# A planner's durations for TensorE products, by width, type and layout of the operands, in a two-block network

## The chip, the cores and the metric

The kernel runs on one core of one Trainium2 chip. The metric is the device time of one execution in microseconds, as the median of several runs. TensorE is called PE here, VectorE DVE, ScalarE ACT, GpSimd POOL, and SyncE SP; SP issues the DMAs.

## The reference

Two transformer-like blocks follow each other on one sequence of 1024 tokens of 1024 features, all in float32.

```python
def hybrid_layer(x, ...):                       # first block
    h = rmsnorm(x, norm1_w)
    proj = h @ w_in                             # q,k,v of two mixers, a gate, two scalars a head
    o_a = gated_delta_rule(qa, ka, va, g, beta) # 4 heads of 128, a recurrence over chunks
    o_b = dilated_attention(qb, kb, vb)         # 8 heads of 64, bands of dilation 1, 4 and 16
    x = x + concat([o_a, o_b]) @ w_out
    u = causal_dwconv(rmsnorm(x, norm2_w) @ w_up, ffn_conv_w)
    return x + (silu(gate) * up) @ w_down       # 2816 wide

def second_block(x, ...):
    proj = rms_norm(x) @ w_in                   # u, v, value, gate: 512 columns each
    a_out = spatial_gating(u_a, v_a, ...)       # chunks of 128 tokens
    b_out = conformer_conv(val_b, gate_b, ...)  # causal convolution with 31 taps, norm, silu
    x = x + concat([a_out, b_out]) @ w_out
    return rms_norm(x + square(relu(rms_norm(x) @ w_ff1)) @ w_ff2)   # 4096 wide
```

## The kernel before

Nearly all products of activations and weights are made in fp32r with operands split into a high and a low part: a product of two float32 matrices is three TensorE products (`mm3`: low x high, high x low, high x high). A tile is 128 rows by 512 columns (half the tokens), one PSUM bank; sums over 1024 features are 24 products. Smaller matrices (the recurrence, the attention's values, the second block's convolution) are multiplied as float32.

**The order is planned at build time.** The program is a set of generator tasks: one for the input projections (`proj1`), one a chunk of the recurrence (`gdn_intra`, with `gdn` for the state), one a head for the scan that finds the attention's maxima (`dil_scan`) and one a head for the attention itself (`dil_pv`), the dense parts (`proj_out`, `ffn`), the convolution (`conv31`, `conv_ln`), and small ones that evacuate a PSUM bank or split a weight. A task yields the engine on which it goes on and a condition. `Weaver.run` (L137) holds a planned clock for each engine. It takes the next task, lets it emit its instructions up to its next yield, and each instruction adds its planned duration to its engine's clock by `cost` (L124). What is emitted is the order of each engine's queue, and the hardware keeps it; nothing of the plan's times is left in the program, only the order and the semaphores.

A TensorE task may be taken if it is due within 50 ns of PE's planned clock, and of those the one with the lowest priority number and then the oldest is taken. A task of another engine is taken if it is due within 100 ns of PE's clock and its engine is planned not more than 2.5 or 6 us ahead (L150). A result passes between engines after a planned latency (`LAT`, L95: 200 ns from PE, 140 from ACT, 130 from DVE) and 230 ns more on the way from ACT or DVE to PE (`TOPE`). The planned durations of ACT, DVE, POOL and DMAs stand in `act`, `tt`, `ts`, `stt`, `ptt` and `dma`: ACT 52 or 94 ns and 0.833 a column, DVE 75 to 130 ns and 1.042 a column, a DMA 475 ns of issue, then 650 ns and its bytes by 360 a nanosecond behind the one before it, and 900 ns to land.

The parts that the steps below go through:

- Projections are filler with high priority numbers (`QP0`, `QP1`, `VP`: 8). `in_steps` (L594) lets go after every two of the eight k, so after six products. `ps_dil` holds q and k of the attention (512 columns), `ps_dv` its v (256 columns).
- The recurrence goes over eight chunks, two in work at a time. A chunk makes some 17 steps between PE and ACT or DVE (`ps_gcb`, `ps_A`, `ps_L`, `ps_T`, `ps_pU`, `ps_G`, `ps_w`), then `gdn` forms `ps_u`, `ps_S`, `ps_o`, and `ps_ot` transposes the result. Its fp32 products appear twice in the records.
- The scan (`ps_S` from arR) and the attention (`ps_T` from arR scores, `ps_O` values) work on heads whose q and k were written to DRAM (`qd`, `kd`) and are read again and split by `dil_split` (L1204) on ACT and DVE, in one queue with the band's additions on DVE and the exponentials on ACT. Six of the eight heads are read twice; two are kept from the scan. Scores of the first pattern use contiguous columns as the stationary operand, those of the second every eighth column (`slice(g + 4 * x, S, 8)`). `dil_pv` keeps three groups of scores ahead (`LA` = 3). The out projection's weights come only after it.
- Buffers come from two arenas; a task that asks for one (`room`) goes on when a planned release has made room.
- In the second block, `conv31` runs 31 taps over 4 groups of channels on DVE; for the last group three taps go to PE (`ps_c`) with diagonal matrices that ACT makes. `conv_ln` then transposes and centres (`ps_ct`), 1500 ns (`CLL`) after the planned end of the taps. `ps_v` and `ps_u` are projections beside it, `ps_sg` the gating, `ps_out` the out projection.

Of the kernel before, what the change touches and what calls it, by code (L numbers as in the profile page):

```python
# [247 lines left out]
def cols(ap):  # L248
    n = 1
    for d in ap.shape[1:]:  # L250
        n *= d
    return n
# [6 lines left out]
class Prog(Weaver):  # L259
# [10 lines left out]

    def mm(self, out, lhsT, rhs, start, stop, loose=False):
        n, m = cols(rhs), cols(lhsT)
        if rhs.dtype == F32:
            c = max(1.667 * n, 213.0 if m > 64 else 107.0)
        elif rhs.dtype == F32R:
            c = max(0.417 * n, 107.0 if m > 64 else 56.0)
        else:
            c = max(0.417 * n, 28.0)
        self.cost("PE", c)
        kw = {"skip_group_check": True} if loose else {}  # L280
        self.nc.tensor.matmul(out, lhsT, rhs, start=start, stop=stop, **kw)  # L281
# [5 lines left out]

    def tp(self, out, in_):
        k = in_.shape[0]
        self.cost("PE", 107.0)  # L290
        self.nc.tensor.transpose(out, in_, self.ident[:k, :k])

    def tpacc(self, out, in_, start):

        self.cost("PE", 107.0)
        self.nc.tensor.matmul(out, in_, self.ident, start=start, stop=True, is_transpose=True, skip_group_check=True)

    def act(self, out, in_, func=AF.Copy, bias=None, scale=None, accum=None):
# [304 lines left out]
    def proj1(self):  # L603
# [49 lines left out]
        for part in range(3):  # L653
            for blk in range(2):
                w = yield from self.pop(q)
                if first:
                    yield "PE", after(*hev[0])
                    self.warm = True
                got = {}
                for mm, hf in ((0, 0), (1, 0), (0, 1), (1, 1)) if first else ((0, 0), (0, 1), (1, 0), (1, 1)):  # L660
                    if first and hf:
                        yield "PE", after(*hev[1])
                    if not hf:
                        got[mm] = yield from rawr.get("PE")
                    h, rs = blk * 2 + mm, got[mm]
                    ps = self.psum("in1")
                    self.gemm_fm(ps, w, mm * P, hT[hf])
                    if not hf:
                        self.cost("POOL", 100.0)
                        nc.gpsimd.memset(rs.ap[:, 0:3], 0.0)  # L670
                    e = self.evac("ACT", lambda d=rs.ap[:, 3 + hf * H:3 + hf * H + H], ps=ps: self.act(d, ps))
                    if hf:
                        posts.append(self.spawn(self.conv4(part, h, rs, rawr, accr, vsr, e), prio=3, eng="DVE"))
                    self.hold = True
                    yield "PE"
                first = False
                self.put(hl, w)
# [1438 lines left out]
```

## Time and profile before

| | |
|---|---|
| median of 3 runs | 2617.27 us (2617.18 to 2620.52) |
| the profiled execution | 2619.11 us |
| its span, first to last instruction | 2617.3 us |
| TensorE busy | 2540.3 us, 97% |
| VectorE, ScalarE, GpSimd busy | 1370.7, 807.9, 121.1 us |
| mean granted clock of TensorE | 0.987 of full speed |

A row of the timeline is a run of like instructions: its start, its length, engine, line, output and inputs, count, and in brackets how long the engine stood before it and what ended that. All matmuls stand on the lines of the helpers (L281 `mm`, L291 `tp`, L296 `tpacc`), so they are told apart by the name of their output. The records of overlapping products are longer than the distance of their starts; the distance is what a product costs. A granted clock of 1.00 is 2.4 GHz, half of it is 1.2 GHz.

### The profile page before, as it was taken

To read this page: it belongs to the slowest core of one execution; us is meant where nothing else is said; L and a number is where in the kernel's file an instruction comes from. 1 tells how busy PE (TensorE), PEld (TensorE's weight loads), DVE (VectorE), ACT (ScalarE), POOL (GpSimd) and SP (SyncE) were. 2 spreads that over 40 slices of the span, in tenths; PEclk is the share of its full clock that TensorE was granted. 3 is DMA by queue.
4 is the path that set the end of the run, shared out by engine and by line. 5 is a ranking of instruction groups with operands and counts; after the bars stand their busy time and mean duration, and the time that the engine had idled before them with its cause. 6 is when DMAs were issued, how large, how long until landed. Compare 5 with 4: busy or idle time off the path is not lost.

```text
span 2617.3 us, 31361 instructions
## 1 busy us (share of the span) xinstructions
PE 2540.3 (97%) x13001; PEld 2180.4 (83%) x13001; DVE 1370.7 (52%) x1868; ACT 807.9 (31%) x1306; POOL 121.1 (5%) x245
## 2 busy tenths in 40 slices
PE   7999999988989999999999999989999999999998
PEld 6888999988978888888888888877788888888887
DVE  5441343454654555555555567969554444444444
ACT  5322443453541422222222235253232121212122
POOL 1010000000000000000000001050000000000000
PEclk9999999998989999999999999999999999999999
DMA  5232222232441111111111113102211111111111
GB/s 189 71 104 85 84 67 62 80 80 69 106 130 57 41 49 49 49 50 50 49 50 49 50 66 101 61 9 90 71 41 57 41 57 41 57 41 57 41 49 65
DMA packets 175164, 170.80 MB, mean 65 GB/s; under 512 B 25985, under 2 KB 148254, under 8 KB 175022
## 3 DMA queue, kind: packets, MB, share of 16 engines
q1 hardware_dynamic: 175022, 168.80, 21.2%
q8 instruction: 102, 1.67, 0.3%
q14 instruction: 40, 0.33, 0.0%
HBM read 145.50 MB, written 23.23 MB: 64 GB/s over the span
## 4 chain that ended last, share of the span: by engine, by line
PE 61%; issue 28%; DVE 4%; ACT 3%; DMA 2%; POOL 2%; SPq 0%; POOLq 0%; ACTq 0%; DVEq 0%
PE ps_up L281 18%; PE ps_dn L281 9%; PE ps_in L281 5%; PE ps_out L281 5%; PE ps_vg L281 3%; PE ps_dil L281 3%; PE ps_T L281 2%; ACT arF L311 2%; PE ps_S L281 2%; PE ps_z L281 2%; PE ps_O L281 2%; PE ps_dv L281 2%; DVE arF L327 2%; PE ps_pU L281 1%; PE ps_G L281 1%
## 5 line engine op out<-in xcount | busy, mean ns | idle before, releaser
L281 PE MATMUL ps_up<-arR 128*128 128x512 f32 x3648 | 831.5, 389 | 0.0
L281 PEld LDWEIGHTS ps_up<-arR 128*128 128x128 f32 x3648 | 684.5, 188 | 142.1
L315 DVE TENSOR_TENSOR arR<-arF,arR 128x1024 fp32r<-128x1024 f32 (+3 forms) x283 | 347.6, 1236 | 610.0 <-ACT arR L311 609.5
L281 PE MATMUL ps_dn<-arR 128*128 128x512 f32 x2592 | 591.8, 389 | 0.0
L311 ACT ACTIVATE arR<-arF 128x1024 fp32r<-128x1024 f32 (+3 forms) x297 | 311.2, 1071 | 852.3 <-PE ps_dn L281 394.3
L281 PEld LDWEIGHTS ps_dn<-arR 128*128 128x128 f32 x2592 | 486.4, 188 | 101.0
L315 DVE TENSOR_TENSOR arF<-arF,ps_dn 128x512 f32<-128x512 f32 x416 | 279.6, 684 | 183.2 <-PE ps_dn L281 183.2
L327 DVE SCALAR_TENSOR_TENSOR arF<-arF,pcol 128x1024 f32<-128x1024 f32 (+1 forms) x276 | 311.4, 1149 | 22.5 <-ACT arF L311 17.5
L311 ACT ACTIVATE arF<-arF 128x1024 f32<-128x1024 f32 (+3 forms) x158 | 134.8, 860 | 272.5 <-DVE arF L315 138.5
L281 PE MATMUL ps_out<-arR 128*128 128x512 f32 x768 | 182.2, 398 | 2.7 <-DVE arR L315 2.7
L281 PEld LDWEIGHTS ps_out<-arR 128*128 128x128 f32 x768 | 146.7, 192 | 34.4 <-DVE arR L315 3.7
L311 ACT ACTIVATE arF<-ps_up 128x512 f32<-128x512 f32 x152 | 89.5, 589 | 187.0 <-PE ps_up L281 187.0
L281 PE MATMUL ps_in<-arR 128*128 128x512 f32 x576 | 137.7, 399 | 0.0
L281 PEld LDWEIGHTS ps_in<-arR 128*128 128x128 f32 x576 | 109.4, 192 | 23.9
L315 DVE TENSOR_TENSOR arF<-arF 128x1024 f32<-128x1024 f32 (+4 forms) x91 | 89.1, 979 | 28.8 <-ACT arF L311 14.8
L281 PE MATMUL ps_dil<-arR 128*128 128x512 f32 x384 | 97.4, 403 | 0.0
L281 PE MATMUL ps_vg<-arR 128*128 128x512 f32 x384 | 88.3, 390 | 0.0
L281 PEld LDWEIGHTS ps_vg<-arR 128*128 128x128 f32 x384 | 71.8, 188 | 14.8
L281 PEld LDWEIGHTS ps_dil<-arR 128*128 128x128 f32 x384 | 71.7, 192 | 14.2
L281 PE MATMUL ps_O<-arF 128*128 128x128 f32 (+2 forms) x384 | 69.9, 328 | 12.2 <-ACT arF L311 6.8
L315 DVE TENSOR_TENSOR arF<-ps_G,csq 128x512 f32<-128x512 f32 x48 | 33.1, 690 | 90.8 <-PE ps_G L281 90.8
L315 DVE TENSOR_TENSOR arF<-arF,ps_out 128x512 f32<-128x512 f32 x64 | 43.5, 683 | 62.1 <-PE ps_out L281 62.1
(185 smaller groups left out, 2037.2 us busy)
## 6 DMA issues: line engine op xcount, KB each, us to landing
arF<-in_w_ff_dram SPq DMA_DIRECT2D x64, 512.0 KB
arF<-in_w_up_dram SPq DMA_DIRECT2D x44, 512.0 KB
arF<-in_w_in_dram SPq DMA_DIRECT2D x12, 1024.0 KB
arF<-in_w_down_dram SPq DMA_DIRECT2D x22, 512.0 KB
arF<-in_x_dram SPq DMA_DIRECT2D x16, 512.0 KB
arF<-in_w_out_dram SPq DMA_DIRECT2D x16, 512.0 KB
arF<-in_w_in_dram SPq DMA_DIRECT2D x16, 512.0 KB
arF<-kd SPq DMA_DIRECT2D x28, 256.0 KB
```

The costliest lines, as they stand in the source:

```text
L281: self.nc.tensor.matmul(out, lhsT, rhs, start=start, stop=stop, **kw)
L311: self.nc.scalar.activation(out, in_, func, **kw)
L315: self.nc.vector.tensor_tensor(out, a, b, op)
L327: self.nc.vector.scalar_tensor_tensor(out, a, s, b, op0, op1)
```

## The change

Four planned durations of TensorE products are replaced. A load figure, 112 ns for a stationary operand of more than 64 columns and 56 otherwise, bounds the cost from below in place of 107 and 56 (twice that for fp32, in place of 213 and 107). 5 ns are added to an fp32 product's 1.667 ns a column, and 13.3 ns to an fp32r product's 0.417 ns a column. An fp32r product whose stationary operand has columns that aren't adjacent in memory counts at least 240 ns. A transpose counts 112 ns in place of 107. The bf16 product's cost stays. No instruction, operand, buffer, priority or latency is edited.

```diff
     def mm(self, out, lhsT, rhs, start, stop, loose=False):
         n, m = cols(rhs), cols(lhsT)
+        load = 112.0 if m > 64 else 56.0
         if rhs.dtype == F32:
-            c = max(1.667 * n, 213.0 if m > 64 else 107.0)
+            c = max(1.667 * n + 5.0, 2.0 * load)
         elif rhs.dtype == F32R:
-            c = max(0.417 * n, 107.0 if m > 64 else 56.0)
+            far = lhsT.ap[-1][0] > 1
+            c = max(0.417 * n + 13.3, 240.0 if far else load)
         else:
             c = max(0.417 * n, 28.0)
         self.cost("PE", c)
...
     def tp(self, out, in_):
         k = in_.shape[0]
-        self.cost("PE", 107.0)
+        self.cost("PE", 112.0)
...
     def tpacc(self, out, in_, start):
 
-        self.cost("PE", 107.0)
+        self.cost("PE", 112.0)
```

## Rows read from the trace of the kernel before

**Rows 1.** The page's first part: busy time, share of the span, instructions.

```profile
span 2617.3 us, 31361 instructions
PE 2540.3 (97%) x13001; PEld 2180.4 (83%) x13001; DVE 1370.7 (52%) x1868; ACT 807.9 (31%) x1306; POOL 121.1 (5%) x245
```

**Rows 2.** Windows by stage: stretch, length, busy (count) by engine, granted clock, DMA.

```profile
core 0: us, PE busy (x) PEld busy (x) DVE busy (x) ACT busy (x) POOL busy (x), PEclk, DMA share, GB/s
0.00:50.00 50.00, 34.27 (x155) 28.57 (x156) 29.14 (x30) 26.45 (x44) 12.49 (x25) 0.90 0.59 205
50.00:200.00 150.00, 150.00 (x809) 129.43 (x808) 66.55 (x60) 48.03 (x58) 12.13 (x11) 1.00 0.27 91
200.00:550.00 350.00, 344.46 (x2491) 324.96 (x2489) 131.65 (x372) 143.02 (x287) 7.87 (x16) 1.00 0.26 76
550.00:640.00 90.00, 74.29 (x566) 71.65 (x567) 43.05 (x124) 39.66 (x84) 6.83 (x12) 0.96 0.19 47
640.00:800.00 160.00, 143.55 (x754) 132.15 (x754) 93.19 (x132) 73.59 (x105) 2.10 (x4) 0.92 0.48 128
800.00:1690.00 890.00, 890.00 (x4030) 740.41 (x4029) 515.14 (x584) 246.63 (x334) 27.21 (x99) 1.00 0.18 54
1690.00:1860.00 170.00, 154.31 (x867) 132.03 (x866) 136.86 (x142) 69.62 (x189) 40.50 (x46) 0.96 0.17 56
1860.00:2600.00 740.00, 740.00 (x3300) 613.82 (x3299) 348.65 (x422) 158.14 (x204) 9.71 (x26) 1.00 0.16 49
2600.00:2617.00 17.00, 9.38 (x42) 7.43 (x40) 6.42 (x7) 2.76 (x6) 2.22 (x6) 0.87 0.23 93
1000.00:1050.00 50.00, 50.00 (x222) 41.42 (x221) 24.98 (x26) 11.10 (x15) 0.30 (x3) 1.00 0.18 53
```

**Rows 3.** Timeline of PE: scan products on adjacent, then on strided columns.

```profile
527.50 0.73 PE L281 MATMUL ps_S<-arR 128*128 128x256 f32 x4
528.07 1.05 PE L281 MATMUL ps_G<-arF 128*128 128x128 f32 x8
...
543.14 1.30 PE L281 MATMUL ps_S<-arR 128*128 128x256 f32 x4
544.26 1.13 PE L281 MATMUL ps_T<-arF 128*128 128x128 f32 x8
```

**Rows 4.** Timeline of PE: fifth chunk's start, last filler, two waits behind it.

```profile
472.60 0.60 PE L296 MATMUL ps_gcb<-csq,g_gc 128*128 128x128 f32 x4
...
513.80 0.95 PE L281 MATMUL ps_dv<-arR 128*128 128x256 f32 x6
...
574.83 1.12 PE L281 MATMUL ps_S<-arR 128*128 128x128 f32 x4 [2.73 <-DVE arR L315]
...
639.14 1.25 PE L291 MATMUL ps_ot<-csq,arF 128*128 128x128 f32 x4 [3.65 <-DVE arF L327]
```

**Rows 5.** ACT's waits from 640 to 800 (total, times, longest); timeline, 721 on.

```profile
ACT arR L311 <- DMA arF<-qd: 7.4, 4, 4.0
...
721.20 1.19 SPq L339 DMA_DIRECT2D arF<-qd  x2
...
727.61 2.00 ACT L311 ACTIVATE arR<-arF 128x1024 fp32r<-128x1024 f32 x2 [4.04 <-DMA arF<-qd]
...
735.68 2.05 PE L281 MATMUL ps_O<-arF 128*128 128x128 f32 x8 [3.50 <-issue]
```

**Rows 6.** Timeline of PE and DVE around the convolution's end, 1690 to 1860 us.

```profile
1689.78 31.48 PE L281 MATMUL ps_v<-arR 128*128 128x256 f32 x261
...
1730.29 5.37 PE L281 MATMUL ps_c<-arF 128*128 128x512 f32 x6 [6.35 <-ACT arF L311]
...
1739.93 2.74 PE L281 MATMUL ps_c<-arF 128*128 128x512 f32 x6
...
1750.41 4.87 DVE L327 SCALAR_TENSOR_TENSOR arF<-arF,pcol 128x1024 f32<-128x1024 f32 x4 [17.50 <-ACT arF L311]
...
1810.99 3.45 PE L281 MATMUL ps_ct<-csq,arF 128*128 128x128 f32 x16 [5.59 <-DVE arF L327]
...
1847.06 2.88 PE L281 MATMUL ps_ct<-csq,arF 128*128 128x128 f32 x16 [2.20 <-DVE arF L327]
```

## The prediction

> **What bounds the kernel now.** I read the page's engine totals first: the reader is to see that TensorE (PE) is busy 97% of the span and no other engine over 52% [rows 1]. Then the stages, one row each: for every stretch I subtract PE's busy time from its length [rows 2]. From 50 to 200 us, 800 to 1690 and 1860 to 2600, nothing is left: PE is never idle there. What it is idle adds up to 76.7 us: 15.7 in the first 50 us (loads and norms, before there is anything to multiply), 5.5 in 200 to 550, 15.7 in 550 to 640, 16.5 in 640 to 800, 15.7 in 1690 to 1860, and 7.6 after the last product. The first and the last have no other work that an order could put there. So at most 53 us, 2% of the span, can be reordered away, plus what the clock costs: in the same three stages the granted clock is 0.96, 0.92 and 0.96 [rows 2], which is 3.6, 12.8 and 6.8 us of full clock given up (0.04 x 90, 0.08 x 160, 0.04 x 170), part of it in the idle time itself.
>
> The change removes no instruction and no byte. It edits durations by which the kernel's own planner lays out the order of instructions; the only thing that can alter the time is another order on the queues.
>
> **The change part by part.** (1) *512-wide fp32r products*, the bulk: planned 213.5 ns, now 226.8 (0.417 x 512 + 13.3). The trace has 222 products in a full 50 us, 225.2 ns each [rows 2], so the new cost is right to 0.7% where the old was 5% short. (2) *256-wide fp32r*: 107, now 120. Four score products whose lhsT is contiguous go by in 0.57 us, 142 each with the change of shape [rows 3]. (3) *Strided lhsT* (every eighth column: half of the scan's and of the attention's scores): 107, now 240; four of them take 1.12 us, 280 each [rows 3]. The old figure was short by more than half. (4) *fp32 of 128 columns and transposes*: 213 to 224 and 107 to 112, 5%. None of these costs a nanosecond itself. What they do is let the planner's PE clock run 5 to 12% faster against ScalarE (ACT), VectorE (DVE) and DMAs, whose planned costs stay. A product that needs such a result is therefore put behind fewer other products than before.
>
> *Saturated stages (50 to 200, 800 to 1690, 1860 to 2600):* 0 us. PE takes one list of products in the order of the weight blocks; it waits for nothing there with the clock at 1.00 [rows 2], while DVE and ACT are busy 515 and 247 of 890 us. The cover is that slack; were it gone, a late block would show as a new wait, and none is there to grow.
>
> *Recurrence and scan, 200 to 640.* Projection products are filler between the steps of the chunk recurrence, six at a time (two k, three products each). A quantum now counts 1.36 us, not 1.28, so a step that comes due is seen at most 0.08 us earlier per quantum. The last filler leaves at 514 us [rows 4]; behind that the idle time begins. From the fifth chunk's start at 473 us [rows 4] (it stands behind buffers that the projections free, so I let costs not move it) 156 products of filler remain, in eleven blocks of which the last is in the row, 26 quanta: 26 x 0.08 = 2 us by which the recurrence can get ahead of its filler, and as much filler saved for the hole. The 3.7 us before the last chunk's transpose [rows 4] stay: nothing else is ready. Against that: one 2.7 us wait is a score product that stands in PE's queue ahead of recurrence work, waiting for a DVE copy of a head [rows 4]; such products move further forward too. I take -2; bounds -8 (half of the stage's idle time) and +5 (that wait doubled and another like it, with no gain).
>
> *Banded attention, 640 to 800.* Per head the planner counted 32 scores x 107 + 14 x 213 + 2 x 213 + 8 x 427 = 10.3 us of PE; now 16 x 120 + 16 x 240 + 16 x 224 + 8 x 432 = 12.8, 25% more. A head's q and k are fetched from DRAM, copied by ACT, and behind those copies on ACT's queue stand the exponentials that PE's value products wait for. The planner lets a pair of fetches land some 3.5 us after issue (0.475 an issue, 0.65, 262144/360 ns each, 0.9). The trace: issued at 721.2, the copy starts at 727.6 after 4.0 us of ACT waiting for qd, and PE then stands 3.5 us [rows 5]. Until now 3.5 planned us covered 25% more real PE work; the copy now goes 0.25 x 3.5 = 0.9 us further forward in ACT's queue, and the wait for the load grows by that. Four such waits, 7.4 us, are in this stage [rows 5], of twelve copies. Bounds: +10 (twelve x 0.9) and -3 (most of the 3.5 us wait goes, if the exponentials are put ahead of the copy). Of the four waits about half reach PE: I take +2.
>
> *Second block's convolution, 1690 to 1860.* DVE is busy 136.9 of 170 us [rows 2]; its 31 taps feed transposing products placed 1.5 us after the planned end. PE waits 6.4 us for ACT's three diagonal copies, then DVE, idle 17.5 us, restarts at 1750.4, and PE waits for its result 5.6 and 2.2 us [rows 6]. From 1750 to 1811 PE is planned 6% slower now: the waiting product moves 60 x 0.06 = 3.6 us forward, and its wait grows so much. But the 256-wide products before it (12% slower in plan) bring ACT's copies forward, 261 products [rows 6] x 13 ns = 3.4 us, and DVE restarts that much earlier. The two nearly cancel. A long hole also costs clock: six half-products take 5.4 us after the 6.4 us wait and 2.7 later [rows 6], so +2.6 us per new hole of that size. I take +1; bounds -8 (both DVE waits go) and +9.6 (3.6 + 3.4 + 2.6).
>
> Sum: 0 - 2 + 2 + 1 = +1 us on a span of 2617.3. The profiled execution took 2619.1, 1.8 us around the span; the median of the three runs is 2617.3, so +1 on that: **2618 us**, no change.
>
> Against the change speaks a rule of the Trainium skill, page "TensorE: Matmul & The Clock Gate", section "Back-to-back issue gap": an isolated product of N columns follows the one before after N/2.4 + 2.5 ns, 216 ns for 512. By it the old 213.5 was nearly right and the new 226.8 is 5% too long; the trace's own spacing disagrees with it here.
>
> **The rivals.** *A, filler is saved (faster).* Recurrence and DVE chain are seen in time, the holes of 550 to 640 and 1690 to 1860 are filled: -8 and -4, attention 0: 2617.3 - 12 = 2605. For it: these stages hold 31 us of idle time [rows 2]. Against it: the 26 quanta are worth only 2 us; it needs the order of the scan heads to fall better as well.
>
> *B, the order trusts loads and DVE too early (slower).* PE was not the only cost planned short: fetches land 6.4 us after issue, not 3.5 [rows 5], and DVE's taps were late by 5.6 us [rows 6] even against a PE that in truth ran 6% slower than planned. That error had been margin; correcting PE alone takes it. Place: ACT's queue in 640 to 800, the same in-order wait as in [rows 5]. Price: 12 copies x 0.9 = 10.4, and 2.6 of clock: +13, 2630. It decides from an ACT wait on a load beyond what the three groups of lookahead hide: 4.0 us of waiting cost PE 3.5, so some 0.5 us is hidden and any growth goes to PE.
>
> *C, hardly anything moves.* A product is taken if due within 50 ns, in quanta of 1.3 us and with fixed priorities; 5% may flip few choices. 2617.3, within 2 us.
>
> *D, the new costs overshoot.* From rows: 226.8 against 225.2 over the 60 us up to 1811 is 0.4 us of waiting, and the strided scores are still 15% short. 2618; what the page's 216 would make of it is B.
>
> **How the numbers follow.** Forecast (sum, within 5 us) 0.26; C 0.08; D 0.02; A 0.31; B 0.33. A measurement of this kernel can tell some 0.2%, 5 us, from no change. Hence faster 0.31, same 0.36, slower 0.33; the three are close because both signs rest on holes of the same 16 us. The forecast's own range is 2612 to 2623. For 8 in 10 it must take in both rivals: the lower bounds -8, -3, -8 combine (squares added, they are not all met at once) to about -12, the upper 5, 10, 9.6 to about +15: 2604 to 2633.
>
> **What would show it.** In the changed kernel: product counts unchanged, 225 ns a product from 800 to 1690, no PE wait there; if one appears, the zero is wrong. Recurrence: the last filler later than 514 us and less than 15.7 us idle in 550 to 640 speaks for A. Attention: ACT's waits for qd and kd above 7.4 us with PE's idle time from 640 to 800 above 16.5 speaks for B; below, against it. Convolution: the waits of 6.4, 5.6 and 2.2 us show whether DVE restarts earlier. Wrong altogether would be an order in which buffers come free in another sequence (the heads' and the recurrence's buffers come from one arena): then a stage would change its length by more than its holes hold.

## The result, and the profile after

| | before | after |
|---|---|---|
| median | 2617.2 us | 2632.0 us |
| after / before | | 1.0057, 95% interval 1.0037 to 1.0076 |
| the profiled execution | 2619.11 us | 2628.86 us |
| its span | 2617.3 us | 2627.1 us |

The changed kernel is slower by 0.57%, some 15 us; its profiled execution happens to be 3 us below its median and the one before 2 us above, so the spans differ by 9.8 us only. All accounts below are made between spans. The first part of the changed kernel's page has the same 13001 products as [rows 1], 2.8 us more of TensorE's time, and 8.1 us more of ACT's:

```profile
span 2627.1 us, 31370 instructions
PE 2543.1 (97%) x13001; PEld 2182.2 (83%) x13001; DVE 1371.6 (52%) x1868; ACT 816.0 (31%) x1312; POOL 122.8 (5%) x245
```

The six more ACT instructions are loads of a function table, which the order decides and the plan doesn't price; before and after:

```profile
L311 ACT ACT_TABLE_LOAD x13 | 16.7, 1283 | 0.9 <-PEq L2101 0.7
...
L313 ACT ACT_TABLE_LOAD x19 | 24.4, 1283 | 1.0 <-PEq L2103 0.7
```

The windows by stage, with the columns of [rows 2]; the last row is one stretch of the row from 800 to 1690 by itself:

```profile
0.00:50.00 50.00, 36.74 (x169) 30.24 (x170) 30.99 (x31) 27.29 (x45) 10.75 (x26) 0.97 0.58 205
200.00:550.00 350.00, 342.92 (x2465) 323.50 (x2465) 139.66 (x402) 137.59 (x281) 7.94 (x16) 1.00 0.26 74
550.00:640.00 90.00, 74.33 (x574) 71.31 (x573) 36.15 (x94) 44.71 (x89) 5.79 (x12) 0.94 0.26 63
640.00:800.00 160.00, 146.23 (x773) 133.89 (x772) 93.55 (x133) 73.32 (x104) 2.10 (x4) 0.94 0.44 122
800.00:1690.00 890.00, 885.32 (x4006) 735.79 (x4006) 520.80 (x590) 246.64 (x334) 29.17 (x99) 1.00 0.18 54
1690.00:1860.00 170.00, 148.25 (x822) 127.97 (x821) 127.17 (x130) 76.46 (x191) 40.19 (x46) 0.92 0.15 53
1860.00:2600.00 740.00, 740.00 (x3299) 613.81 (x3299) 346.68 (x418) 156.92 (x200) 9.16 (x22) 1.00 0.15 47
...
1560.00:1690.00 130.00, 125.32 (x621) 105.42 (x620) 104.94 (x131) 56.33 (x89) 16.19 (x34) 1.00 0.26 85
```

Length minus PE's busy time, against [rows 2], gives the account: -2.5 us idle in the first 50 us (13.3 for 15.7), +1.5 in 200 to 550, nothing in 550 to 640, -2.7 in 640 to 800 (13.8 for 16.5), **+4.7 in 1560 to 1690** (before: none), **+6.1 in 1690 to 1860** (21.8 for 15.7), +0.1 at the end: +7.2. With the 2.8 us by which the same products took longer, it makes 10.0 us, for a measured 9.8. The granted clock from 1690 to 1860 is 0.92, before 0.96. In the first part the changed kernel gains: the first product of `ps_up` (its first block's second half) starts 5.6 us earlier than before (859.6 for 865.2 us). By the last of `ps_dn` it is 9.9 us late. So the second block's entry and convolution lose 15.5 us, more than the whole difference.

Where PE stands in that stretch, in the changed kernel. First its timeline at the second block's entry; a row is a run of like products with its start and length, and in brackets how long PE stood before it and for whom:

```profile
1572.99 0.49 PE L293 MATMUL ps_tr<-csq,arF 128*128 128x128 f32 x3
1574.92 3.39 PE L293 MATMUL ps_tr<-csq,arF 128*128 128x128 f32 x29 [1.44 <-ACT arF L313]
1578.06 8.46 PE L283 MATMUL ps_dn<-arR 128*128 128x512 f32 x36
1586.35 11.05 PE L283 MATMUL ps_vg<-arR 128*128 128x512 f32 x48
1597.24 3.65 PE L293 MATMUL ps_tr<-csq,arF 128*128 128x128 f32 x32
1603.96 5.70 PE L283 MATMUL ps_vg<-arR 128*128 128x512 f32 x24 [3.07 <-DVE arR L317]
```

and the same stretch before, where nothing waits (its first row is cut at the window's start):

```profile
1564.81 16.71 PE L281 MATMUL ps_dn<-arR 128*128 128x512 f32 x73
1581.36 3.65 PE L291 MATMUL ps_tr<-csq,arF 128*128 128x128 f32 x32
1584.77 5.70 PE L281 MATMUL ps_dn<-arR 128*128 128x512 f32 x24
1590.31 16.49 PE L281 MATMUL ps_vg<-arR 128*128 128x512 f32 x72
1606.63 3.65 PE L291 MATMUL ps_tr<-csq,arF 128*128 128x128 f32 x32
```

The same blocks in the same sequence, but the first transposes stand 12 products (2.7 us) further forward among the down projection's, and the second 24 products (5.4 us) further forward among `ps_vg`: ahead of what ACT and DVE can have ready. Next the convolution's stage, the changed kernel's PE:

```profile
1717.34 1.25 PE L293 MATMUL ps_cb<-csq,arF 128*128 128x128 f32 x4 [6.85 <-ACT arF L313]
...
1734.94 1.25 PE L293 MATMUL ps_cb<-csq,arF 128*128 128x128 f32 x4 [1.93 <-ACT arF L313]
1737.25 1.25 PE L293 MATMUL ps_cb<-csq,arF 128*128 128x128 f32 x4 [1.06 <-ACT arF L313]
...
1766.92 5.75 PE L283 MATMUL ps_u<-arR 128*128 128x512 f32 x24 [0.63 <-DVE arR L317]
1774.11 5.78 PE L283 MATMUL ps_u<-arR 128*128 128x512 f32 x24 [1.43 <-DVE arR L317]
...
1790.98 3.78 PE L283 MATMUL ps_ct<-csq,arF 128*128 128x128 f32 x16 [4.75 <-DVE arF L329]
...
1836.28 3.76 PE L283 MATMUL ps_ct<-csq,arF 128*128 128x128 f32 x16 [5.10 <-DVE arF L329]
```

`ps_cb` is the transpose behind the root in `conv_ln`. Behind its 6.85 us the timelines of POOL, ACT and DVE show this:

```profile
1706.01 8.74 POOL L370 TENSOR_SCALAR ms<-bss 128x4 f32<-128x4 f32 x1 [50.66 <-ACT arF L313]
1714.83 2.05 POOL L372 TENSOR_TENSOR brs<-ms,nhalf 128x4 f32<-128x4 f32 x1
...
1716.92 1.14 ACT L313 ACTIVATE arF<-ps_ct,brs 128x128 f32<-128x128 f32 x4 [10.63 <-POOL brs L372]
...
1705.04 25.50 DVE L329 SCALAR_TENSOR_TENSOR arF<-arF,pcol 128x1024 f32<-128x1024 f32 x20
```

POOL's step over 4 columns, planned at 128 ns, lies 8.74 us beside DVE's taps; ACT waits 10.6 us for it, and PE, whose queue has the transposes next, 6.85.

### The profile page after: what moved, and what is told of

It is laid out like the page before. It is cut to its first block, busy times and chain, and to the rows that moved or that the text cites. A ratio compares the mean times of both kernels' runs of the same rounds, so it can differ in the third digit from the quotient of the medians.

```text
span 2627.1 us, 31370 instructions
## 1 busy us (share of the span) xinstructions
PE 2543.1 (97%) x13001; PEld 2182.2 (83%) x13001; DVE 1371.6 (52%) x1868; ACT 816.0 (31%) x1312; POOL 122.8 (5%) x245
## 4 chain that ended last, share of the span: by engine, by line
PE 61%; issue 28%; DVE 4%; ACT 3%; POOL 2%; DMA 2%; SPq 0%; POOLq 0%; ACTq 0%; DVEq 0%
PE ps_up L283 18%; PE ps_dn L283 8%; PE ps_out L283 6%; PE ps_in L283 5%; PE ps_dil L283 3%; PE ps_vg L283 3%; PE ps_T L283 3%; ACT arF L313 2%; PE ps_S L283 2%; PE ps_z L283 2%; PE ps_pU L283 2%; PE ps_O L283 2%; PE ps_G L283 1%; PE ps_dv L283 1%; DVE arF L329 1%
## 5 line engine op out<-in xcount | busy, mean ns | idle before, releaser
L329 DVE SCALAR_TENSOR_TENSOR arF<-arF,pcol 128x1024 f32<-128x1024 f32 (+1 forms) x276 | 311.9, 1150 | 20.5 <-ACT arF L313 15.5
```

What stands on the lines that cost most here:

```text
L329: self.nc.vector.scalar_tensor_tensor(out, a, s, b, op0, op1)
```

## The experiments

Two theories. **Lost margin:** the products were planned 5% shorter than they are, so PE in truth reached a waiting product later than the plan had it, and that hid what the plan has too short or not at all on other engines. Correcting the products alone puts every product that needs another engine's result too far forward. Where the plan is short shows in the rows: it is not the plain steps of DVE and ACT (where the records of taps overlap, one of 1024 columns every 1.20 us, planned 1.197; two ACT copies in 2.00 us [rows 5], planned 1.89), but POOL's step (8.74 us, planned 0.13), the taps that don't overlap (1.32 us) and the table loads (1.28 us each, not planned). Rival, **chance:** any other set of numbers gives another order, and its time has nothing to do with the direction of the edit. In the runs below, most edits act only behind `mid1`, a point just ahead of the first block's last down projection (about 1500 us); ahead of it these kernels have the changed kernel's order (e2 the old one). Each ratio is to runs of the kernel before beside it, whose medians were 2615.9 to 2618.1 us. What each run showed, with PE's idle time (stretch minus busy, from its own windows) in the two stretches and the granted clock in the second (two traces of one order, before and e1 or after and e2, agree to 0.4 us of idle time):

| run | us | ratio to before (95%) | idle 1560 to 1690 | idle 1690 to 1860 | clock there |
|---|---|---|---|---|---|
| before | 2617.2 | | 0.0 | 15.7 | 0.96 |
| after | 2632.0 | 1.0057 (1.0037 to 1.0076) | 4.7 | 21.8 | 0.92 |
| e1_new_then_old | 2614.0 | 0.9981 (0.9972 to 0.9991) | 0.0 | 16.1 | 0.96 |
| e2_old_then_new | 2633.8 | 1.0056 (1.0041 to 1.0071) | 4.7 | 21.7 | 0.92 |
| e3_others_106 | 2622.5 | 1.0015 (1.0006 to 1.0024) | 0.0 | 23.1 | 0.92 |
| e4_cll_8 | 2618.3 | 0.9999 (0.9989 to 1.0008) | 4.7 | 13.6 | 0.96 |
| e5_old_tail_cll_8 | 2617.4 | 1.0003 (0.9993 to 1.0013) | 0.0 | 21.3 | 0.93 |
| e6_wide_7 | 2622.1 | 1.0019 (1.0010 to 1.0029) | 2.8 | 16.2 | 0.93 |
| e7_wide_27 | 2637.0 | 1.0075 (1.0060 to 1.0090) | 11.0 | 18.7 | 0.93 |
| e8_wide_m13 | 2623.9 | 1.0028 (1.0018 to 1.0039) | 2.3 | 21.5 | 0.93 |
| e9_pool_4 | 2616.7 | 1.0001 (0.9992 to 1.0011) | 4.6 | 12.3 | 0.95 |
| e10_rstd_act | 2631.4 | 1.0061 (1.0044 to 1.0078) | 4.6 | 22.5 | 0.94 |
| e11_wide_15 | 2631.0 | 1.0067 (1.0048 to 1.0085) | 4.7 | 26.9 | 0.91 |
| e12_pool_4_cll_8 | 2614.8 | 0.9987 (0.9978 to 0.9996) | 4.6 | 10.6 | 0.97 |

**Where the loss sits: e1 and e2.** The change is split in time: new costs up to `mid1` and old ones behind it, and the reverse.

```diff
+        if self.old:
+            if rhs.dtype == F32:
+                c = max(1.667 * n, 213.0 if m > 64 else 107.0)
+            elif rhs.dtype == F32R:
+                c = max(0.417 * n, 107.0 if m > 64 else 56.0)
...
         def mid1():
+            self.old = True
```

The second has `self.old` true from the start and `False` at `mid1`.

> The new durations up to the first block's last down projection (some 1500 us), the old ones behind it. The profiles put the changed kernel 5.6 us ahead of the kernel before at the first up projection and 9.9 behind at the end. If the whole loss is made in the second block's convolution stage, this one keeps the head start and none of the loss: 2617 - 5.6 = 2611.6 us, between 2609 and 2614. If the loss belongs to the new order in the first part and only shows later, about 2632.

> The old durations up to the same place, the new ones behind it. If the convolution stage makes the loss: 2617 + 15.5 = 2633 us. If the first part makes it: 2617.

Measured 2614.0 and 2633.8: the second as expected, the first at the upper end of its range. The first half of the change by itself makes the kernel faster by 0.2%; the second half loses 16 us (e2 against the kernel before) to 18 (the changed kernel against e1). e1's waits of PE (total, times, longest) behind 1540 us are those of [rows 6], to the tenth:

```profile
PE ps_ct L289 <- DVE arF L335: 7.8, 2, 5.6
PE ps_c L289 <- ACT arF L319: 6.4, 1, 6.4
```

**Margin or chance: e3.** The new costs throughout, and behind `mid1` the planned durations and latencies of all other engines longer by 6.3%, so that all engines are planned in the old proportion.

```diff
...
     def cost(self, eng, ns):
+        if eng != "PE":
+            ns *= self.slow
...
         def mid1():
+            self.slow = 1.063
```

> The new durations throughout, and from the first block's last down projection on the planned durations of the other engines and the latencies between engines made longer by 6.3% too (226.8 / 213.5). If the lost margin is the cause (TensorE corrected alone, the others left short), the margin is back: the waits of the convolution stage fall to those of the kernel before, 15.7 us idle in 1690 to 1860 us and no wait before 1690; 2612 us like the kernel with old durations there. If any other order than the old one loses there by chance, it stays between 2620 and 2635.

Measured 2622.5 us: inside what chance alone was given (2620 to 2635), and 10 us above what margin alone would give (2612). Its windows of PE show the two stretches part company:

```profile
1560.00:1690.00 130.00, 130.00 (x667) 1.00 0.28 88
1690.00:1860.00 170.00, 146.88 (x814) 0.92 0.16 53
```

At the second block's entry the idle time is gone, as the margin theory says. In the convolution it is 23.1 us, no better than in the changed kernel; PE now waits 8.4 us at `ps_c` and 13.9 at the two `ps_ct`. The scaling leaves `CLL`, the lookahead windows and the priorities as they were; that this is why the old order isn't restored there was not tested.

**One cover made longer: e4 and e5.** `CLL`, the time from the planned end of the taps to the centring products, 8 us in place of 1.5: behind the new costs (e4), and from `mid1` on behind the old ones (e5).

```diff
-    ISSUE, N1P, SSL, CLL = 475.0, 2, 6000.0, 1500.0
+    ISSUE, N1P, SSL, CLL = 475.0, 2, 6000.0, 8000.0
```

> The changed kernel with the transposing products of the convolution placed 8 us, not 1.5 us, behind the planned end of the taps. In the changed kernel these products wait for VectorE 4.75 and 5.10 us. If they stand too early in TensorE's queue, both waits go and 10 us with them: 2622. If VectorE itself is what the stage waits for, the wait moves to the next product that needs it, and the time stays at 2632.

> New costs until just ahead of the first block's last down projection, the old ones behind it (as in e1_new_then_old, 2614.0 us, span 2613.5), and from there the lead that a product's readers are given (CLL) is 8000 ns in place of 1500. What it asks: is what CLL bought behind the new costs (e4_cll_8: the two waits for ct, 4.75 and 5.10 us, gone; 13.7 us in all) there behind the old costs too? If the waits for ct are a thing of the priority that the norm's readers get, with the old costs too, then its waits for ct (5.6 and 2.2 us in the kernel before) go and the time is 2614 - 7.8 = 2606 us. If CLL only made good what the new costs had spoilt, the time stays at 2614 us (2611 to 2617).

e4 took 2618.3 us, 14 below the changed kernel, where 10 were expected. Both waits for `ps_ct` are gone, and PE's waits behind 1540 us are now, in all:

```profile
PE ps_cb L293 <- ACT arF L313: 12.2, 5, 5.0
PE ps_vg L283 <- DVE arR L317: 3.2, 2, 3.1
PE ps_c L283 <- ACT arF L313: 1.5, 1, 1.5
PE ps_tr L293 <- ACT arF L313: 1.4, 1, 1.4
```

The same step behind the old costs bought nothing and cost 3 us (e5 2617.4 us, against e1's 2614.0): there too the waits for `ps_ct` went, but the one at `ps_c` grew from 6.4 to 13.8 us and `ps_out` got 8.7. So the longer lead is no gain of its own; it gained only in the order that the new costs had made. My 2606 was wrong: I had taken the wait away and left its successor out.

**Dose: e6, e7, e8, e11.** The 13.3 ns that the change adds to a contiguous fp32r product is 6.65, 26.6, -13.3 and 15.0 ns behind `mid1`.

```diff
-            c = max(0.417 * n + 13.3, 240.0 if far else load)
+            c = max(0.417 * n + self.wide, 240.0 if far else load)
...
         def mid1():
+            self.wide = 6.65
```

> The changed kernel, but from ahead of the first block's last down projection on the term added to a contiguous fp32r product is 6.65 ns in place of 13.3 (a 512-wide one planned at 220 ns in place of 227). Margin theory (planned products shorter than real ones left the slower engines slack, and the change took it): half the slack is back, so the time lies between the changed kernel's 2632 and the 2614 of e1_new_then_old, about 2623 us (2617 to 2629). Chance theory (any other number gives another order, and its time has nothing to do with the direction): anywhere from 2612 to 2634 us, with no order among this run, e7_wide_27 and e8_wide_m13.

> The same term at 26.6 ns (a 512-wide product planned at 240 ns, about 15 ns longer than the trace shows it) from ahead of the first block's last down projection on. Margin theory: the products seem longer still, the readers of their results are planned earlier than they can be, and the waits behind the two norms of the convolution stage grow: above 2632 us, about 2645 by the slope of 18 us on 13.3 ns. Chance theory: anywhere from 2612 to 2634 us.

> The same term at -13.3 ns (a 512-wide product planned at 200 ns, 25 ns shorter than the trace shows it; the shortest bounds as in the changed kernel) from ahead of the first block's last down projection on. Margin theory: more slack than the old costs gave, so no wait behind a norm is longer than in the kernel before: at most 2614 us. Chance theory: anywhere from 2612 to 2634 us; above 2625 us would speak against the margin theory by itself.

> The changed kernel with the term added to a contiguous fp32r product at 15.0 ns in place of 13.3 from ahead of the first block's last down projection on: a 512-wide product planned at 228.5 ns in place of 226.8, less than 1 per cent. As a size this is nothing, yet some 24 rows of TensorE's order change in the convolution stage. If the time follows how long the products seem, it lies within 2 us of the changed kernel's 2632 (2630 to 2635). If each new order is a draw of its own, it lies 4 us or more away on either side, between 2612 and 2637 us.

On the long side the times rise with the term: 2614.0 (e1, whose other three costs are the old ones too), 2622.1, 2632.0, 2631.0, 2637.0 for 0, 6.65, 13.3, 15 and 26.6 ns. e7's 2637.0 is above the 2634 that chance was given, and below the 2645 that the slope gave. The run with the shorter products (e8, 2623.9) speaks against margin as the whole of it: it should have been at 2614 or below and is 10 us above. By stretch the picture is cleaner on the long side: at the second block's entry the idle time follows the dose, 0.0, 2.8, 4.7, 4.7, 11.0. On the short side it doesn't: e8 has 2.3 us there, a wait of `ps_tr` for ACT, where margin wants none. In the convolution it follows nothing: 16.1, 16.2, 21.8, 26.9, 18.7, and 21.5 for -13.3. e11 differs from the changed kernel by 1.7 ns a product and has the same total, but PE stands elsewhere; its timelines of PE and POOL:

```profile
1721.12 1.25 PE L294 MATMUL ps_cb<-csq,arF 128*128 128x128 f32 x4 [16.60 <-ACT arF L314]
...
1700.04 18.49 POOL L371 TENSOR_SCALAR ms<-bss 128x4 f32<-128x4 f32 x1 [44.90 <-ACT arF L314]
```

**POOL in the plan, and POOL on the chip: e9 and e10.** e9 only tells the planner that the norm's root on POOL takes 4 us longer. e10 takes the work itself away from POOL: ACT makes the root in one instruction (with its shorter planned time PE's order changes behind 1707 us too).

```diff
+        self.cost("POOL", 4000.0)
         self.rstd(r, ss, 1.0 / P)
         yield "ACT"
```

```diff
-        yield "POOL"
-        self.rstd(r, ss, 1.0 / P)
-        yield "ACT"
+        self.rstd_act(r, ss, 1.0 / P)
...
+    def rstd_act(self, out, ss, scale):
+        self.act(out, ss, AF.Abs_reciprocal_sqrt, scale=scale, bias=self.epst)
```

> The changed kernel with one planned duration more: the root of the convolution's norm on POOL is planned 4 us longer than it was (planned at 1.1 us; in the changed kernel's trace the first of these pairs of instructions took 8.74 + 2.05 us beside the taps on DVE, and TensorE waited 6.85 us behind it). If an order that trusts POOL too early is the cause of that wait, the transposes behind this norm come 24 to 48 products of 256 columns later (2.9 to 5.8 us), the wait of 6.85 us shrinks to 1 to 4 us, and the time is 2626 us (2623 to 2629). If what one wait gives back another one takes, the time stays at 2632 us with the idle time of 1690 to 1860 us at its 21.8 us.

> The changed kernel with the root of the convolution's norm taken by ACT (one activation that gives the reciprocal root) in place of two instructions on POOL; each of them may bring a load of ACT's function table (1.28 us a piece in the trace) and the result can differ in the last digits. Nothing of this norm stands on POOL any more. If POOL's 8.74 us beside DVE's taps is what TensorE waits for at 1717 us, that wait (6.85 us) goes: 2632 - 6.9 = 2625 us (2622 to 2628). If DVE's taps or ACT's queue are behind it, a wait of 5 us or more stays at the first transposes of this norm and the time is 2630 to 2634 us.

e10 took the wait away and won nothing. PE's three longest waits behind 1540 us in e10:

```profile
PE ps_ct L283 <- DVE arF L329: 13.1, 2, 6.9
PE ps_cb L293 <- ACT arF L313: 5.0, 4, 2.6
PE ps_u L283 <- DVE arR L317: 3.6, 1, 3.6
```

The first `ps_cb` waits 0.4 us, not 6.85, but `ps_ct` waits 13.1 (9.9 in the changed kernel) and `ps_u` 3.6: PE, let go earlier, runs into DVE's taps, and the idle time stays at 22.5 us. I expected 2625 if POOL was the cause of that wait. It was, and the time stayed at 2631: another result stood behind the wait. The run isn't clean, though: each root on ACT brings a table load, 27 loads for 19, and ACT is busy 88.1 us from 1690 to 1860 for 76.5, so part of what the wait gave may have gone there. e9, which alters no work at all, took 2616.7 us, 15 below the changed kernel and more than the 6 I expected. Its two longest waits:

```profile
PE ps_ct L283 <- DVE arF L329: 7.0, 2, 4.3
PE ps_cb L293 <- ACT arF L313: 5.4, 2, 4.5
```

POOL still takes 9.27 us for that step there; what changed is the order, in which PE waits 5.4 us for 9.8 at the `ps_cb`, 7.0 for 9.9 at `ps_ct` and not at all at `ps_u`.

**Both corrections: e12.** e9 with e4's `CLL`.

> The changed kernel with both planned durations corrected: the root of the convolution's norm on POOL 4 us longer (e9_pool_4, 2616.7 us) and the lead from DVE's taps to the norm's products 8 us in place of 1.5 (e4_cll_8, 2618.3 us). The first leaves two waits for ct (7.0 us in all) and 4.5 us at the first transposes behind the norm; the second took the waits for ct to nothing and left 12.2 us at such transposes. If each correction takes away its own wait (TensorE's order trusts the engine that it follows too early), both groups go, idle time in 1690 to 1860 us falls from 12.3 to about 5 us, and the time is 2609 us (2605 to 2612), below both kernels. If the waits only change places, the time stays between 2614 and 2620 us with 12 us or more of idle time there.

Measured 2614.8 us, ratio 0.9987 (0.9978 to 0.9996): under both kernels, but not the 2609 I hoped for; against e1 it isn't told apart. The waits for `ps_ct` are gone and idle time is the least of all runs, 10.6 us at a clock of 0.97. Two of 5.1 and 4.1 us stay at `ps_cb`: POOL's first step takes as long as before (9.85 us), and 4 us of plan don't cover it. e12 also settles a rival, the table loads: it has 19 of them like the changed kernel (13 before), and loses nothing, so the loads by themselves are not the loss.

## Where the prediction was wrong, and where it was right

The time fell inside the range of 2604 to 2633, 1 us from its upper end, and that is in part luck: the upper bound was added up from three stages, two of which gained, while a stage priced at nothing lost. (By its own sum the lower end is 2606; nothing hangs on it.) The forecast of no change was wrong: the kernel is slower, with a chance of 0.33 given. Point by point:

- *Saturated stages, 0 us.* Wrong in one place. 225 ns a product held (222 products from 1000 to 1050 again, as in [rows 2]), and up to 1560 and from 1860 PE waits for nothing. From 1560 to 1690 it stands 4.7 us. The step that failed is "the cover is that slack": I argued from DVE's and ACT's busy share over 890 us, and the cover of a norm is not the share but how many products stand between two blocks in PE's queue; there the plan moved 12 and 24 of them away. The text named this case (a late block would show as a new wait) and priced it at nothing.
- *Recurrence and scan, -2 us.* By the windows it is +1.5. The last block of `ps_dv` filler did go later, from 514 us [rows 4] to 557 us, yet the idle time of 550 to 640 is 15.67 us for 15.71. But 1.9 us of it now are a wait of the attention for its load of `mf`, which ended at 642.8 us before (2.2 us) and so stood in the next row of the table. Without it these holes did shrink by 2 us; against that, others opened in 200 to 550, one of them 1.6 us at a `ps_dv` that waits for DVE, and -0.4 is left:

```profile
505.18 5.92 PE L283 MATMUL ps_dv<-arR 128*128 128x256 f32 x48 [1.60 <-DVE arF L317]
...
556.59 3.09 PE L283 MATMUL ps_dv<-arR 128*128 128x256 f32 x24
...
638.84 4.39 PE L283 MATMUL ps_T<-arR 97*128 97x256 f32 x19 [1.93 <-DMA arR<-mf]
```

- *The first 50 us, left out of the sum.* I said no order could put other work there. It gained 2.5 us: before, 40 transposes stood ahead of the first product of `ps_in`, now 32, and it starts at 20.2 us, not 24.8.
- *Banded attention, +2 us.* The sign is wrong: it is -2.7, or -0.7 with the wait for `mf` counted here in both kernels. ACT's waits for `qd` and `kd` (total, times, longest) got shorter, not longer; before they were 7.4 us in four for `qd` [rows 5] and 4.2 in one for `kd`, which the text left out:

```profile
ACT arR L313 <- DMA arF<-qd: 5.8, 3, 3.6
...
ACT arR L313 <- DMA arF<-kd: 4.1, 1, 4.1
```

  I had moved the copy forward in ACT's queue and held the fetch still. In the changed kernel the last pair goes out at 718.5 us and its copy starts 9.9 us later, without a wait; before it started 6.4 us behind the issue, after 4.0 us of waiting [rows 5]. So that copy moved back, not forward. The 3.5 us of PE that I put on that wait were never shown to be its: the row gives "issue" for them, time in which PE waits for nothing that the profile shows. One trace is a rough measure here: the twelve traces with the new order ahead of 1500 us have 28.1 to 31.3 us idle from 550 to 800, the two with the old one 32.2 and 33.2. So for the recurrence's end and the attention together the sign holds, the size to some 3 us.
- *Second block's convolution, +1 us.* This is the mis-sized term: with the entry it cost 15.5 us, of which 10.7 are idle time and the rest, by that account, longer products. I followed one chain, DVE's restart and the product that waits for it. DVE restarts at 1746.0 us, 4.4 earlier than [rows 6] (I said 3.4), and the two `ps_ct` together wait 9.9 us for 7.8: that cancellation was about right. But it counted shifts of a few products, and the order moved by blocks: the first of these `ps_ct` starts at 1791 us, not 1811, and 96 products of `ps_u` and `ps_out` that stood ahead of it now stand behind (21.6 us at 225 ns). By outputs, PE's waits from 1540 us on changed so: `ps_ct` +2.1, `ps_c` and `ps_cb` together +2.9 (9.8 for 6.9, now behind POOL's step, which the sum doesn't mention), `ps_vg` +3.2, `ps_tr` +1.4, `ps_u` +1.7, `ps_out` -0.7: +10.6. No one of them is the loss. DVE's restart in the changed kernel:

```profile
1746.02 4.87 DVE L329 SCALAR_TENSOR_TENSOR arF<-arF,pcol 128x1024 f32<-128x1024 f32 x4 [15.47 <-ACT arF L313]
```

- *Rival A* needs 8 us less idle time in 550 to 640 and 4 in 1690 to 1860. The first came to 2, the second turned into a loss. Its gain is real only in the first part of the kernel, and about half of it stands where it named none, in the first 50 us: e1 is 0.19% faster.
- *Rival B* had the number (2630) and the mechanism (a plan that trusts the slower engines too early, with products no longer planned short as cover), and the wrong place: not the loads behind ACT's queue in the attention but the norms of the second block. At its entry the runs bear it out for longer products: the idle time follows the planned length and goes when all engines are planned in proportion; for products planned shorter still it fails (2.3 us in e8). In the convolution they show half: two planned times made longer (POOL's root, the lead behind DVE's taps) give back 15 and 14 us each; but the idle time there doesn't follow the dose, shorter products don't help, and with orders that differ by 20 us a part of either gain may be chance. Each order there is partly a draw of its own, and of the twelve orders of the second half that were timed the old one is, with e12's, the best.
- *D, the overshoot.* The Trainium skill's page "TensorE: Matmul & The Clock Gate", section "Back-to-back issue gap", has 216 ns for an isolated product of 512 columns. e6 planned 220, near to that, and lay between. The runs can't turn that into a verdict on the product's true length, which the trace gives as 225.

What stays open: why PE's total idle time in the convolution is so nearly the same in the changed kernel, e10 and e3 while the waits that make it up differ (21.8, 22.5, 23.1 us); why e9's one number brought 15 us and not 6; and why e8, with shorter products, waits at the entry.

## What to carry to other kernels

When a planner lays out the order, the errors of its durations are tied together: correcting one engine alone can take away the cover under every other engine that is planned too short. Look for those first (here a step planned at 0.13 us that takes 8.7), and time the result stage by stage: splitting the change at a point of the program found a gain in one half that the other half's loss had hidden. And a wait that is taken away on the chip is only a gain if the next result in PE's queue is already there; a longer time in the plan, which moves the waiting products, was worth 15 us where taking the step off POOL, at the price of table loads on ACT, was worth nothing.

## What the runs showed of the hardware

A POOL instruction over 4 columns takes 0.19 us where DVE stands still, and 8.74, 9.27, 9.85 and 18.49 us as the first one beside DVE's chain of taps in the changed kernel, e9, e12 and e11; later ones take 0.2 to 2.6 us. The Trainium skill's page "SBUF — State Buffer", section "Who interferes with whom", says that a DVE instruction with two inputs in SBUF contends with a GpSimd instruction that reads SBUF. The traces agree with the direction; a wait as long as 7 to 15 taps they add to it. It is not the norm's root alone: the first POOL instruction there is another one, over 1 column, in the kernel before, and took 6.77 us.

What ends the long wait can be read from DVE's records. The changed kernel's taps behind 1705 us, and the POOL step of the same form once DVE stands still:

```profile
1705.04 9.65 DVE L329 SCALAR_TENSOR_TENSOR arF<-arF,pcol 128x1024 f32<-128x1024 f32 x8
1714.73 15.82 DVE L329 SCALAR_TENSOR_TENSOR arF<-arF,pcol 128x1024 f32<-128x1024 f32 x12
...
1733.20 0.19 POOL L370 TENSOR_SCALAR ms<-bss 128x4 f32<-128x4 f32 x1 [1.97 <-ACT arF L313]
```

A tap's record is 1.28 us long. The first eight start every 1.20 us, each 0.08 us before the record ahead of it ends; the last twelve start every 1.32 us, 0.04 us after it ends. POOL's 8.74 us end at 1714.75 us, with the first tap that starts after such a gap. So it is in all thirteen traces that have such a wait (4.3 to 18.5 us long): no gap falls inside it, and it ends within 0.1 us of the first DVE instruction behind one. In e10 POOL's instruction began at 1716.44 us, 0.2 us ahead of the first gap, and took 0.33 us. The gap is not the whole rule: further on, among overlapping taps, POOL's instructions got through in 2.0 to 2.6 us without one. Why the spacing changes was not tested; by the count of taps, the last twelve may be one group's chain left alone, in which each tap needs the one before. DVE's pace doesn't follow POOL: it is 1.20 us while POOL is held up, and 1.32 us from 1717 to 1722 us, where POOL does nothing.
